# Shift and scale vectors of a two-block network: eight products with a column of ones in place of eight transposes and two VectorE sums

## The chip, the cores and the metric

One core of a Trainium2 chip runs the whole program. The metric is the device time of one execution in microseconds (us); smaller is better. The kernel before took 1699.3 us, the median of three runs (1696.49, 1699.3 and 1700.89). Three engines matter here: TensorE (PE in the rows; PEld is its weight load, which runs beside the product before it), VectorE (DVE) and ScalarE (ACT). GpSimd is POOL, SyncE is SP.

## The reference

The program is two networks in a row on an input x of 256 rows and 1024 columns, all in float32. The first has two blocks (an attention and gating mixer, then a convolution mixer), each followed by an MLP; the second is one block (attention with selection, then a feed-forward layer over many experts). What the change touches is the modulation, the same in each block:

```python
m = (silu(c) @ w_mod[l] + b_mod[l])[:, None, :]        # 6 * 1024 numbers
sh1, s1, g1, sh2, s2, g2 = jnp.split(m, 6, axis=-1)
h = rmsnorm(x, norm_g) * (1 + s1) + sh1                # ahead of the mixer
x = x + g1 * mixer(h)
h = rmsnorm(x, norm_g) * (1 + s2) + sh2                # ahead of the MLP
x = x + g2 * mlp(h)
```

c is one vector of 1024 numbers, so each of the six results is a vector of 1024.

## The kernel before, in words

A modulation vector is made in two stages. In `mod_steps` (line 286) POOL clears a tile t of 128 partitions by 2048 columns (line 294) and brings the bias into its first partition by a DMA (line 296); then eight steps follow, one per block k of 128 rows of the modulation weights. A step loads 128x1024 weights (line 142) and VectorE adds weights times silu(c) to t (line 306, `scalar_tensor_tensor`). Row p of t then holds the part of the sum that came from input rows p, p+128 and so on; what is left is a sum over the 128 partitions.

That last sum takes two forms. A gate (g1, g2) is wanted as a row that is the same on all partitions: `mod_row` (line 322) multiplies a 128x128 tile of ones by t (line 328) and ScalarE copies the result (line 329). A shift or a scale (sh, s) is wanted with its 1024 numbers down the partitions, as a tile of 128 partitions by 8 columns: that is `mod_cols` (line 310). For each of two halves it takes a PSUM tile `ps`, transposes four 128x128 blocks of t into it (line 318, `nc.tensor.transpose` with the identity `self.ident`), and VectorE sums each block along its columns (line 319, `tensor_reduce`). In a transpose and in a product alike, the block of t is the stationary operand that PEld loads; in a transpose the 128 columns of the identity stream past it.

`mod_cols` is called ten times: for sh2 and s2 of the first block from `steps` inside the attention mixer (`mixer0_rest`, lines 716 to 870), and eight times from `mod_groups` (line 335), whose `last` step (line 342) calls `mod_result` (line 332) for the two vectors of a group. `mod_groups` serves the two MLPs (`mlp`, line 592): in each, six vectors for what comes later are made between the products of the MLP itself, four of them by `mod_cols`.

The tiles named `ps` share eight PSUM banks; a tile that wants a bank waits until an earlier one has been read. The results go through `mod_scale` (line 394) for a scale, and are then read in `highs` (lines 425 and 427), where the normalised rows are scaled and shifted.

Around it: each weight matrix is brought in blocks, ScalarE makes its high part (line 172) and VectorE its low part (line 173), and every product is three matmuls, high by high, high by low and low by high (lines 179 to 181). In the attention mixer a score product (line 787) is followed by VectorE's sum with the bias and its minimum (line 627), ScalarE's exponential (line 629), VectorE's division (lines 632 and 634), transposes (line 803), copies (line 804) and value products (line 809).

The program's instructions are put into one queue per engine by a planner at build time. It prices each instruction and may send one ahead of another that stands earlier in the source when its operands are ready by its own clock, so the queues need not have the source's order. Each engine takes its queue in order.

Of the kernel before, what the change touches and what calls it, by code (L numbers as in the profile page):

```python
# [15 lines left out]
OP = mybir.AluOpType  # L16
AX = mybir.AxisListType
PSUM = bass.MemoryType.PSUM

P = 128  # L20
# [50 lines left out]
class Net:  # L71
# [238 lines left out]
    def mod_cols(self, t, half, name):  # L310

        nc = self.nc
        m = self.const([P, 8], name=name)
        for q in range(2):
            pt = self.ps([P, 4, P])
            for j in range(4):
                o = half * 1024 + (q * 4 + j) * P
                nc.tensor.transpose(pt[:, j, :], t[:, o : o + P], self.ident)
            nc.vector.tensor_reduce(m[:, q * 4 : q * 4 + 4], pt, axis=AX.X, op=OP.add)
        return m  # L320

    def mod_row(self, t, half):
# [1241 lines left out]
```

## Time and profile before

| | us |
|---|---|
| median of three runs | 1699.3 |
| profiled execution | 1695.26 |
| its span in the trace | 1693.5 |
| TensorE busy in the span | 1624.9 (96%) |
| VectorE busy | 1273.5 (75%) |
| ScalarE busy | 833.6 (49%) |
| GpSimd busy | 168.8 (10%) |
| granted TensorE clock, mean | 0.986 of full |

The span runs from the first to the last instruction of the trace, and 1.76 us of the profiled execution lie around it. Busy shares are means over stages with different limits, so what counts for an edit is the stage in which it lies. Matmuls are pipelined: the duration of one (273 ns, say) is longer than the distance at which the next one starts (0.11 us in the same run of instructions), so costs on TensorE are read from the distances between starts.

### The profile page before, as it was taken

What the parts mean: (1) busy time and instruction counts of PE and PEld (TensorE: products, weight loads), DVE (VectorE), ACT (ScalarE), POOL (GpSimd) and SP (SyncE); (2) the same over time, 40 slices, a digit from 0 to 9 for tenths busy, and PEclk for the clock granted to TensorE, in tenths of its full rate; (3) what the DMA queues carried; (4) which work ended last, traced back from release to release, by engine and by line L of the source; (5) the groups of instructions that cost most, each with busy time, mean ns of one, the idle gap of its engine ahead of it and who ended that gap; (6) DMA issues with size and microseconds to landing.
All of it is one profiled execution on the core that took longest, in us unless ns stands there. A gap on an engine that the chain in (4) does not pass through costs nothing.

```text
span 1693.5 us, 27346 instructions
## 1 busy us (share of the span) xinstructions
PE 1624.9 (96%) x10518; PEld 1444.4 (85%) x10518; DVE 1273.5 (75%) x2042; ACT 833.6 (49%) x1229; POOL 168.8 (10%) x133
## 2 busy tenths in 40 slices
PE   7998999999968999999989999999999999999998
PEld 4875898988857988886789999999999998888886
DVE  7887688876966888947869888988845556776665
ACT  6546545442126455646644455555554444444444
POOL 0110100000001000000047770000000000000001
PEclk9999999999979999999999999999999999999999
DMA  9783499956415999474166666777786668999970
GB/s 376 267 286 125 147 345 344 339 178 221 139 38 206 365 330 349 164 263 149 59 230 203 216 210 231 275 250 252 255 285 218 211 214 281 336 315 324 320 252 34
DMA packets 145397, 406.63 MB, mean 240 GB/s; under 512 B 13169, under 2 KB 46065, under 8 KB 143090
## 3 DMA queue, kind: packets, MB, share of 16 engines
q1 hardware_dynamic: 137280, 390.66, 67.0%
q10 hardware_dynamic: 7474, 14.16, 2.2%
q8 instruction: 82, 1.34, 0.3%
q14 instruction: 49, 0.40, 0.1%
q0 software_dynamic: 512, 0.07, 0.0%
HBM read 374.43 MB, written 30.41 MB: 239 GB/s over the span
## 4 chain that ended last, share of the span: by engine, by line
PE 75%; issue 10%; DVE 3%; ACT 2%; DMA 1%; POOL 1%; SPq 0%; POOLq 0%; DVEq 0%; ACTq 0%
PE ps L179 7%; PE ps L181 7%; PE ps L180 7%; PE pa L179 7%; PE pa L181 7%; PE pa L180 7%; PE acc L180 7%; PE acc L181 7%; PE acc L179 7%; PE acc L1309 3%; PE ps L588 2%; PE ps L894 2%; DVE m L885 1%; DMA st<-w_ff 1%; PE ps L1171 1%
## 5 line engine op out<-in xcount | busy, mean ns | idle before, releaser
L172 ACT CAST hi<-st 128x1024 fp32r<-128x1024 f32 x466 | 474.3, 1046 | 444.7 <-PE pa L180 169.6
L173 DVE TENSOR_TENSOR lo<-st,hi 128x1024 fp32r<-128x1024 f32 (+1 forms) x416 | 495.5, 1219 | 176.2 <-ACT hi L172 170.7
L179 PE MATMUL pa<-k,hi 128*128 128x256 f32 x1024 | 289.4, 283 | 0.0
L180 PE MATMUL pa<-k,hi 128*128 128x256 f32 x1024 | 286.3, 280 | 0.0
L181 PE MATMUL pa<-k,lo 128*128 128x256 f32 x1024 | 286.3, 280 | 0.0
L179 PE MATMUL ps<-k,hi 128*128 128x256 f32 x816 | 230.0, 283 | 0.0
L180 PE MATMUL ps<-k,hi 128*128 128x256 f32 x816 | 229.4, 281 | 0.0
L181 PE MATMUL ps<-k,lo 128*128 128x256 f32 x816 | 229.4, 281 | 0.0
L179 PE MATMUL acc<-hi,m 128*128 128x512 f32 x512 | 199.7, 390 | 0.0
L180 PE MATMUL acc<-lo,m 128*128 128x512 f32 x512 | 199.3, 389 | 0.1
L181 PE MATMUL acc<-hi,m 128*128 128x512 f32 x512 | 199.3, 389 | 0.0
L180 PEld LDWEIGHTS pa<-k,hi 128*128 128x128 f32 x1024 | 194.1, 190 | 0.5
L181 PEld LDWEIGHTS pa<-k,lo 128*128 128x128 f32 x1024 | 193.4, 189 | 0.0
L179 PEld LDWEIGHTS pa<-k,hi 128*128 128x128 f32 x1024 | 192.3, 188 | 0.5
L179 PEld LDWEIGHTS ps<-k,hi 128*128 128x128 f32 x816 | 154.2, 189 | 3.4 <-issue 1.0
L181 PEld LDWEIGHTS ps<-k,lo 128*128 128x128 f32 x816 | 156.2, 191 | 0.6 <-DVE lo L173 0.5
L180 PEld LDWEIGHTS ps<-k,hi 128*128 128x128 f32 x816 | 154.9, 190 | 2.1 <-issue 0.5
L173 POOL TENSOR_TENSOR lo<-st,hi 128x1024 fp32r<-128x1024 f32 x50 | 119.0, 2406 | 35.4 <-ACT hi L172 26.1
L306 DVE SCALAR_TENSOR_TENSOR k<-st,sil,k 128x1024 f32<-128x1024 f32 x96 | 117.6, 1280 | 0.0
L181 PEld LDWEIGHTS acc<-hi,m 128*128 128x128 f32 x512 | 96.1, 188 | 20.3 <-DVE m L195 0.4
L180 PEld LDWEIGHTS acc<-lo,m 128*128 128x128 f32 x512 | 96.1, 188 | 20.1 <-DVE lo L173 0.5
L179 PEld LDWEIGHTS acc<-hi,m 128*128 128x128 f32 x512 | 96.1, 188 | 19.6 <-issue 0.2
(298 smaller groups left out, 2623.4 us busy)
## 6 DMA issues: line engine op xcount, KB each, us to landing
st<-w_ff SPq DMA_DIRECT2D x128, 512.0 KB, 6.1
st<-uT SPq DMA_DIRECT2D x128, 512.0 KB, 4.6
st<-v SPq DMA_DIRECT2D x128, 512.0 KB, 5.3
st<-w_mod SPq DMA_DIRECT2D x96, 512.0 KB, 5.9
st<-w_ada SPq DMA_DIRECT2D x48, 512.0 KB, 5.9
st<-w_in SPq DMA_DIRECT2D x44, 512.0 KB, 5.7
gates<-k SPq DMA_DIRECT2D x16, 1024.0 KB, 7.4
k<-gates SPq DMA_DIRECT2D x16, 1024.0 KB, 8.5
```

The costliest lines, as they stand in the source:

```text
L172: nc.scalar.copy(h, raw)
L173: self.last_lo = (lo or nc.vector).tensor_tensor(l, raw, h.bitcast(F32), op=OP.subtract)
L179: mm(ps, l.hi, r.hi, start=first, stop=False)
L180: mm(ps, l.hi, r.lo, start=False, stop=False)
L181: mm(ps, l.lo, r.hi, start=False, stop=last)
L306: nc.vector.scalar_tensor_tensor(t[:, s], st, by, t[:, s], op0=OP.mult, op1=OP.add)
L588: mm(p[:, j, :], wt[k][:, j * P : (j + 1) * P], h[:, k, :], start=k == 0, stop=k == KC - 1)
L885: nc.vector.scalar_tensor_tensor(v, z[:, i : i + T], self.col("w_dw", c * 31 + i), v, op0=OP.mult, op1=OP.add)
L894: nc.tensor.matmul(yt[t][c % 2][:, c // 2 * P : c // 2 * P + P], z[:, t * P + i : t * P + i + P], dg[:, i, :], start=i == 0, stop=False)
L1171: nc.tensor.matmul(po[64 * i : 64 * i + 64, c * P :], v[:, c, (hd - 1 + i) * 64 : (hd + i) * 64], pTs[hd - 1 + i][:, 2 * c : 2 + c, :], st ...
L1309: nc.tensor.matmul(pg[:, i, :], y[:, q + i, :], z[:, q + i, :], start=True, stop=True)
```

## The change

Only `mod_cols` is changed. One PSUM tile of 128x8 takes the place of two tiles of 128x512; eight float32 matmuls, each with a block of t as stationary operand and the first column of the tile of ones as moving operand, take the place of eight transposes; each gives one column of the result, already summed over the partitions. One VectorE copy of 128x8 takes the place of two sums. The order of allocations in SBUF stays as it was (one `const` tile per call).

```diff
     def mod_cols(self, t, half, name):
 
         nc = self.nc
+        pt = self.ps([P, 8])
+        for j in range(8):
+            o = half * 1024 + j * P
+            nc.tensor.matmul(pt[:, j : j + 1], t[:, o : o + P], self.ones[:, 0:1], start=True, stop=True)
         m = self.const([P, 8], name=name)
-        for q in range(2):
-            pt = self.ps([P, 4, P])
-            for j in range(4):
-                o = half * 1024 + (q * 4 + j) * P
-                nc.tensor.transpose(pt[:, j, :], t[:, o : o + P], self.ident)
-            nc.vector.tensor_reduce(m[:, q * 4 : q * 4 + 4], pt, axis=AX.X, op=OP.add)
+        nc.vector.tensor_copy(m, pt)
         return m
```

## Rows read from the trace of the kernel before

**Rows 1.** Windows: stretch, us, busy PE PEld DVE ACT POOL (count), granted clock, DMA share, GB/s.
```profile
196.00:372.00 176.00, 175.49 (x1138) 158.65 (x1137) 146.61 (x140) 89.94 (x120) 2.77 (x3) 1.00 0.86 308
545.00:700.00 155.00, 155.00 (x1000) 140.09 (x1000) 132.28 (x124) 78.12 (x101) 2.77 (x3) 1.00 0.93 342
```

**Rows 2.** Line 318 alone: count, ns min/median/max, first and last start us, shape.
```profile
L318 PEld LDWEIGHTS ps<-ident,k x64: 139/141/143, 261.2 to 691.7; 128*128 128x128 f32 x64
L318 PE MATMUL ps<-ident,k x64: 272/273/273, 261.6 to 691.8; 128*128 128x128 f32 x64
```

**Rows 3.** Timeline of one MLP call: start us, us, engine, line, operation, count.
```profile
643.12 1.04 PE L318 MATMUL ps<-ident,k 128*128 128x128 f32 x8
643.99 1.88 PE L328 MATMUL ps<-k,ones 128*128 128x512 f32 x4
...
642.89 1.03 PEld L318 LDWEIGHTS ps<-ident,k 128*128 128x128 f32 x8
...
643.76 1.29 DVE L319 TENSOR_REDUCE s<-ps 128x4 f32<-128x512 f32 x2 [0.62 <-PE ps L318]
```

**Rows 4.** Groups by line: busy us, mean ns of one, idle before.
```profile
L319 DVE TENSOR_REDUCE s<-ps 128x4 f32<-128x512 f32 x10 | 6.5, 683 | 1.2 <-PE ps L318 1.2
L319 DVE TENSOR_REDUCE sh<-ps 128x4 f32<-128x512 f32 x10 | 6.4, 685 | 4.2 <-PE ps L318 4.2
```

**Rows 5.** Timeline of line 259: float32 products with two moving columns.
```profile
52.41 1.05 PE L259 MATMUL ps<-pairs,m 4*128 4x2 f32 x8
53.38 0.39 PE L179 MATMUL ps<-k,hi 128*128 128x256 f32 x1
```

**Rows 6.** Timeline of line 894: loads for full-height float32 products, 128 moving columns.
```profile
456.28 3.65 PEld L894 LDWEIGHTS ps<-diag,z 128*128 128x128 f32 x32 [1.69 <-issue]
```

**Rows 7.** Groups: weight loads of 4 and of 128 columns.
```profile
L248 PEld LDWEIGHTS ps<-m,silq 128*4 128x4 f32 x64 | 5.1, 88 | 11.0 <-DVE m L244 3.3 <-issue 1.7
...
L259 PEld LDWEIGHTS ps<-pairs,m 4*128 4x128 f32 x32 | 3.9, 186 | 3.8 <-DVE m L256 3.5 <-issue 0.4
```

**Rows 8.** Groups: a small VectorE instruction that reads PSUM.
```profile
L263 DVE TENSOR_TENSOR mc<-ps,cols 128x4 f32<-128x4 f32 x8 | 0.9, 158 | 3.3 <-PE ps L259 3.3
```

**Rows 9.** Timeline at the first attention call.
```profile
110.78 1.04 PE L318 MATMUL ps<-ident,mod 128*128 128x128 f32 x8
111.63 1.28 DVE L319 TENSOR_REDUCE sh<-ps 128x4 f32<-128x512 f32 x2
111.75 1.99 PE L787 MATMUL ps<-b,b 64*128 64x512 f32 x8
111.88 0.95 POOL L294 MEMSET mod<- 128x1024 f32 x1 [11.47 <-PE ps L318]
112.91 0.69 DVE L627 CUSTOM_DVE_ANT_1 m<-ps,bias 128x512 f32<-128x512 f32 x1
113.12 0.55 POOL L296 DMA_DIRECT2D mod<-b_mod  x1 [0.29 <-POOL mod L294]
113.66 0.19 PEld L179 LDWEIGHTS ps<-k,hi 128*128 128x128 f32 x1 [0.76 <-DVE sm L627]
...
116.52 1.29 DVE L306 SCALAR_TENSOR_TENSOR mod<-st,sil,mod 128x1024 f32<-128x1024 f32 x1 [0.83 <-POOL bias L780]
```

**Rows 10.** Instructions that use the tile `mod`: time of its DMAs to landing.
```profile
DMA to landing us min/median/max: 3.3/3.7/4.3
```

**Rows 11.** Timeline at the second attention call.
```profile
150.66 0.44 PE L318 MATMUL ps<-ident,mod 128*128 128x128 f32 x2
...
151.02 1.08 PE L809 MATMUL ps<-m,b 128*64 128x256 f32 x6
...
152.03 0.87 PE L318 MATMUL ps<-ident,mod 128*128 128x128 f32 x6
```

**Rows 12.** Chain of waits behind that call: start us, us, what.
```profile
153.43 1.07 ACT m L804 x2
...
158.31 2.35 DVE b L173 x2
```

## The prediction

> **What bounds the kernel now.** I read the busy shares first, then the stages in which the ten calls of `mod_cols` lie, then the neighbourhood of a call, then rows of like instructions for what the change adds. TensorE is busy for 96% of the span and VectorE for 75%. Eight of the ten calls lie in the two MLPs, four in each, the first from 261.6 us, the last with its last transpose at 691.8 [rows 2]. In the stretches that hold them TensorE is busy for 175.49 of 176.00 us and for 155.00 of 155.00 us at the full clock, while VectorE has 29.4 and 22.7 us to spare [rows 1]. The reader is to see that in these stretches only TensorE's own time counts: taking work from VectorE can win at most the 0.5 us in which TensorE is idle. The other two calls lie in the attention mixer, at 111 and 151 us, where several engines take turns in holding the others up.
>
> **What it removes.** 80 transposes and 20 sums. The transposes of one MLP call start at 643.12 and the next product starts at 643.99, so eight take 0.87 us, 0.109 each, though each lasts 0.273 [rows 2, 3]; 80 are 8.7 us of TensorE. The sums are 6.5 + 6.4 = 12.9 us of VectorE [rows 4].
>
> **What it adds to TensorE.** 80 float32 products of a 128x128 block of t with one column. The stationary block is the same as before; what goes is 127 of the 128 columns that stream past. So the question is what sets the distance from one product to the next, the stream or the load of the next block. The trace has no product with one column. The nearest rows are line 259's, with two columns: eight start from 52.41 and the next product follows at 53.38, 0.121 each with the change of operands at the end, and 0.114 within (1.05 for eight, less the last one's quarter microsecond, over seven) [rows 5]. They hold four partitions instead of 128, but 128 columns of weights, at the full clock. With all 128 partitions and 128 moving columns, line 894 loads 32 blocks in 3.65 us: less the last load's 0.19 that is 3.46 over 31, or 0.112 each [rows 6]. A plain load of 128 columns lasts 0.186 and one of four columns 0.088 [rows 7], so the 128 columns themselves take about 0.10: loads one behind the other make 0.11 whatever streams beside them. A transposing load is shorter, 0.141 [rows 2], which by the same subtraction is 0.053 of columns, and there it was the stream that made the 0.109. I take 0.112, nearest in partitions and in weights: 80 x (0.112 - 0.109) = +0.2 us. The ends are 0.121 (line 259 with its change-over, +1.0 us) and 0.053 (if plain loads came as fast as transposing ones, -4.5 us). TensorE is thus relieved of nothing: the stream that the change takes away was as long as the load that stays.
>
> Against this the Trainium skill has a rule (TensorE: Matmul & The Clock Gate, Back-to-back issue gap): a moving operand of 1 to 64 columns takes about 60 cycles, some 25 ns, from one product to the next, against 134 cycles at 128 columns. Its section LDWEIGHTS on the same page gives a load of 128 columns as 128/1.2, or 107 ns. By the first alone the 80 products would save 80 x (0.109 - 0.025) = 6.7 us; by the second nothing. Line 259's 0.114 speaks for the second.
>
> **What it adds to VectorE.** Ten copies of 128x8 out of PSUM. The nearest row reads 128x4 from PSUM and takes 0.158 [rows 8]: 1.6 us in all, so VectorE is relieved of 12.9 - 1.6 = 11.3 us, 9 of them in the MLPs, where its slack already covers everything. The copy waits for the eighth product where the first sum waited for the fourth transpose; behind it on VectorE stand the low parts of weights (line 173). At 643 the sums end at 645.0 [rows 3]; the copy would start at about 643.12 + 7 x 0.112 + 0.27 = 644.2 and end at 644.4, so those low parts come earlier, not later. TensorE did not wait for them before either.
>
> **PSUM.** A call takes one bank for a short while instead of two for longer, so no product waits longer for a bank. In the MLPs there is no such wait to remove, since TensorE is never idle.
>
> **The first attention call.** The two sums keep VectorE from 111.63 to 112.91, and then line 627 starts, though it needs only the first pair of the eight score products (line 787) that run from 111.75 to 113.74; by an estimate (a third of their 1.99 us) that pair was done at about 112.4. TensorE's next load comes at 113.66 and had waited 0.76 for line 627 [rows 9]. Here up to 0.5 us is to be had for both. It goes no further, however: the next step of the modulation (line 306) starts at 116.52 after VectorE had idled for 0.83 [rows 9]. The row names POOL, but POOL's bias DMA was issued at 113.12 and such DMAs take 3.3 to 4.3 us to land [rows 9, 10], so it was the landing, 116.4 or later. That DMA follows POOL's clearing of the tile at 111.88, which waits for the last transpose, and the last product ends at the same time as that. So VectorE meets the same landing again, and what it saved is idle time ahead of it. I take 0.1 us, with 0 and 0.5 as ends.
>
> **The second attention call.** TensorE does two transposes at 150.66, six value products, and six transposes at 152.03 [rows 11]; the chain then passes through ScalarE's copies (line 804) and later through VectorE's low part at 158.31 [rows 12]. The sums (0.68 each) are not on it. Fewer banks held may bring the transposes of line 803 forward; I take 0.2 us, with 0 and 0.7 (the time that one sum holds a bank longer) as ends.
>
> **Moves.** No DMA, POOL or SP instruction is added, removed or reordered in the source. The planner, however, puts the queues in order by its own clock, and it does leave the source's order: the eight transposes of one call stand in the queue as two and six around six products of line 809 [rows 11]. With cheaper steps it may choose other orders from 110 us on. In the MLPs an other order costs nothing while TensorE stays full. At stage ends it can shift a wait: the 2.35 us of the two low parts at 158.31 [rows 12] are one such wait, which may go or come again elsewhere, so I allow 2.4 us to either side.
>
> **The sum.** +0.2 - 0.1 - 0.2 = -0.1 us on the profiled execution's 1695.26. That execution lies 4.0 us below the median of 1699.3, and the three runs lie between 1696.5 and 1700.9; a change of -0.1 on the median gives 1699.2 us. A change of under 0.3% (5.1 us) can't be told from none with such runs.
>
> **Rivals.**
> 1. The products are cheaper than the load (loads hidden behind each other, or as fast as transposing ones). For it: 0.053 of columns in a transposing load [rows 2, 7]. Against it: lines 259 and 894 [rows 5, 6]. It gives -4.5 us at 0.053 each, 1694.8, so close to the 5.1 that with the spread of the runs half of it would be told as faster. Chance 0.06. By the page's rule on small moving operands above it would be 1692.6.
> 2. Slower: a plain float32 product can't overlap with the load of the next block as a transpose does. Each pair then costs 0.19 for the load alone, 80 x (0.19 - 0.109) = +6.5 us, 1705.7; with the product's 0.27 behind it, 0.46 and +28 us, 1727. It decides from 0.173 each, where 80 x 0.064 makes 5.1 us, and it sits where TensorE is full, with nothing to hide it. Against it are the 0.112 of line 894, plain, full height, a new load each [rows 6]. Chance 0.05. The Trainium skill has a rule that speaks for this rival (TensorE: Matmul & The Clock Gate, Terms): the transposing mode is four times faster for float32. By it a plain product would stand at 4 x 0.109 = 0.44, near the upper price; line 894's 0.112 against 0.109 disagrees.
> 3. The planner's new order decides, by over 5.1 us one way or the other, at stage ends that this trace can't foretell. Chance 0.10, half each way.
> 4. The 11.3 us of VectorE turn up in the time after all, because VectorE is what holds up the attention mixer: 1699.3 less at most the 1.2 us (0.5 and 0.7) of the two calls there, so this can't leave the bound of no change. It is part of the forecast.
>
> **How the numbers follow.** Forecast 0.79, rivals 0.06, 0.05 and 0.10. Faster by over 0.3%: 0.03 of rival 1 and 0.05 of rival 3, and 0.02 for the forecast's own tail, together 0.10. Slower: 0.05 and 0.05, together 0.10. Within: 0.80. The range joins the ends: down 4.5 (loads) and 1.2 (attention) from 1699.3, 1693.6; up 1.0 (change-over) and 2.4 (order), 1702.7, rounded up to 1703 for the spread of the runs.
>
> **What would show it.** In the profile after: ten groups of eight products in place of line 318 with 0.11 from start to start, loads of 0.19; ten VectorE copies of about 0.16 and VectorE some 11 us less busy; TensorE still full in both MLPs; line 306's start near 116.5 still tied to the bias DMA. The prediction is wrong if the products stand at 0.06 or at 0.19, if gaps open on TensorE in the MLPs, or if the stages after 180 us differ by more than 2 us with the same work.

## The result, and the profile after

| | before | after |
|---|---|---|
| median of four runs of each, us | 1697.89 | 1713.66 |
| lowest and highest, us | 1696.35 to 1700.89 | 1710.71 to 1715.89 |
| profiled execution, us | 1695.26 | 1711.66 |
| its span, us | 1693.5 | 1709.9 |
| TensorE busy, us | 1624.9 | 1641.8 |
| VectorE busy, us | 1273.5 | 1264.0 |
| granted TensorE clock, mean | 0.986 | 0.979 |

The change makes the kernel slower: ratio 1.0104, 95% interval 1.0081 to 1.0127. The prediction of 1699.2 us and its range (to 1703.0) are missed.

Lines of the changed kernel are one lower than before behind the change: the products stand on line 316, their copy on 318, the products of low parts still on 181, the relu on 600. First the page's line on the engines, then line 316 in the view of one line (count; ns minimum, median, maximum; first and last start; shape), and the copies from the groups by line:

```profile
PE 1641.8 (96%) x10598; PEld 1460.1 (85%) x10598; DVE 1264.0 (74%) x2032; ACT 834.3 (49%) x1229; POOL 168.8 (10%) x133
...
L316 PEld LDWEIGHTS ps<-ones,k x128: 187/192/193, 261.9 to 704.5; 128*128 128x128 f32 x128
L316 PE MATMUL ps<-ones,k x128: 165/250/251, 262.3 to 704.5; 128*128 128x1 f32 x128
L316 PEld LDWEIGHTS ps<-ones,mod x32: 186/192/193, 109.3 to 149.6; 128*128 128x128 f32 x32
L316 PE MATMUL ps<-ones,mod x32: 167/250/271, 109.7 to 149.6; 128*128 128x1 f32 x32
```

The reader is to see the counts. The source makes 80 products; the trace has 128 + 32 = 160 pairs of load and matmul. Before, the eight MLP calls had 64 records for 64 transposes [rows 2]. A product of two plain float32 operands is executed here as two passes, each with a load of its own; a transpose is one.

The second MLP call of the first MLP, in time (start, length, engine, line, count); it answers to [rows 3]:

```profile
308.29 1.84 PE L316 MATMUL ps<-ones,k 128*128 128x1 f32 x16
309.99 1.96 PE L327 MATMUL ps<-k,ones 128*128 128x512 f32 x4
...
310.17 0.17 DVE L318 COPY s<-ps 128x8 f32<-128x8 f32 x1 [1.85 <-PE ps L316]
310.37 0.17 DVE L393 SCALAR_TENSOR_TENSOR sm<-s,cols 128x8 f32<-128x8 f32 x1
310.45 1.22 DVE L173 TENSOR_TENSOR lo<-st,hi 128x1024 fp32r<-128x1024 f32 x1
```

Sixteen passes occupy TensorE from 308.29 to 309.99, 1.70 us or 0.106 a pass, 0.21 a product. The eight transposes of such a call occupied 0.87. VectorE's part of the call came out as forecast (0.17 a copy instead of 1.3 for two sums).

Each MLP has three calls: two for one vector and, last, one for two (sh2 and s2, "the double call"). This is what VectorE and TensorE do at the first double call, and then the same place in 2 us windows (length; busy time and count on PE, PEld, DVE, ACT, POOL; granted clock; DMA share; GB/s):

```profile
355.98 3.63 PE L316 MATMUL ps<-ones,k 128*128 128x1 f32 x32
359.47 0.36 PE L179 MATMUL ps<-k,hi 128*128 128x256 f32 x1
359.67 0.28 PE L180 MATMUL ps<-k,hi 128*128 128x256 f32 x1
361.01 0.58 PE L181 MATMUL ps<-k,lo 128*128 128x256 f32 x1 [1.06 <-DVE lo L173]
...
357.86 0.17 DVE L318 COPY sh<-ps 128x8 f32<-128x8 f32 x1 [3.28 <-PE ps L316]
359.65 0.17 DVE L318 COPY s<-ps 128x8 f32<-128x8 f32 x1 [1.62 <-PE ps L316]
359.73 1.22 DVE L173 TENSOR_TENSOR lo<-st,hi 128x1024 fp32r<-128x1024 f32 x1
```

```profile
356.00:358.00 2.00, 2.00 (x20) 2.00 (x19) 0.14 (x1) 2.00 (x3) 0.00 (x0) 1.00 1.01 414
358.00:360.00 2.00, 1.95 (x17) 1.75 (x16) 0.38 (x3) 0.35 (x1) 0.00 (x0) 1.00 0.39 160
360.00:362.00 2.00, 0.99 (x4) 0.99 (x5) 2.00 (x3) 0.00 (x0) 0.00 (x0) 0.52 0.12 18
362.00:364.00 2.00, 2.00 (x12) 2.00 (x11) 2.00 (x3) 0.00 (x0) 0.00 (x0) 0.50 0.78 225
364.00:366.00 2.00, 2.00 (x11) 2.00 (x11) 2.00 (x3) 0.00 (x0) 0.00 (x0) 0.50 0.73 246
366.00:368.00 2.00, 2.00 (x16) 2.00 (x15) 0.71 (x1) 0.00 (x0) 0.00 (x0) 0.77 0.13 45
```

Three things come together. The run of passes is 3.49 us long (355.98 to 359.47; the 16 transposes took 1.66). The copy of the second vector stands in VectorE's queue ahead of a low part of weights (line 173); VectorE idles 1.62 us for it, the low part starts at 359.73, and TensorE waits 1.06 us for that part. And behind the run the granted clock drops from 1.00 to 0.50, the 1.2 GHz level: by its means in the windows (0.52 and 0.77) from 360.1 to 366.9, 6.8 us, in which 11 or 12 products fall into a window of 2 us where cols128 below has 20. At 360.1 TensorE had been waiting for only 0.1 us, so the clock falls at the start of the wait and not behind it. Before, the same stage ran at 1.00 from end to end [rows 1].

**Where the 16.4 us lie.** ScalarE's relu and VectorE's last sum of an MLP (`m<-ps,grow`, line 459 before) come in the same number in both kernels, so their starts can be subtracted. First MLP, after minus before: 0.72 at its start, 0.71 ahead of the first call, 1.41 behind it, 2.08 behind the second, 7.88 at its end (387.42 against 379.54). Second MLP: 9.46 at its start, 9.60 ahead of the calls, then 10.31, 10.97, and 17.12 at its end. At the end of the kernel it is 16.4. So the four single calls cost 0.70 each, the double calls 5.80 and 6.15, and the stage between the MLPs 1.6. The 0.7 ahead of the first MLP is not the price of the two attention calls: at the end of that mixer (line 459's sum, at 187.27 in before) after is 0.95 ahead. It loses 1.7 from there to the first relu, where its granted clock is at 0.50 from 192.8 to 196.2 and that of before at 1.00; turncopy below, which keeps the transposes, has the same fall at 192.6 and loses the same 1.7. For the double calls the end of the MLP is the mark, since the next relu is misleading there: before, four later products had been drawn ahead of it.

### The profile page after: what moved, and what is told of

Same layout as the page of the kernel before. It is cut to its first block, busy times and chain, and to the rows that moved or that the text cites. A ratio compares the mean times of both kernels' runs of the same rounds, so it can differ in the third digit from the quotient of the medians.

```text
span 1709.9 us, 27500 instructions
## 1 busy us (share of the span) xinstructions
PE 1641.8 (96%) x10598; PEld 1460.1 (85%) x10598; DVE 1264.0 (74%) x2032; ACT 834.3 (49%) x1229; POOL 168.8 (10%) x133
## 4 chain that ended last, share of the span: by engine, by line
PE 75%; issue 10%; DVE 3%; ACT 1%; DMA 1%; POOL 1%; SPq 0%; POOLq 0%; ACTq 0%; DVEq 0%
PE ps L179 7%; PE ps L181 7%; PE ps L180 7%; PE acc L181 7%; PE acc L179 7%; PE acc L180 7%; PE pa L179 7%; PE pa L181 7%; PE pa L180 7%; PE acc L1308 3%; PE ps L587 2%; PE ps L893 1%; DVE m L884 1%; PE ps L1170 1%; PE ps L316 1%
```

## The experiments

Delays in this table are worked out in the same way against the trace of before: single call (mean of the four), first and second double call, and what the stage between the MLPs adds. "L510" is how long the eight products of the bias row in that stage take (line 510 before), which tells the clock there.

| kernel | ratio to before | single | double 1 | double 2 | between | L510 |
|---|---|---|---|---|---|---|
| after | 1.0104 [1.0081, 1.0127] | 0.70 | 5.80 | 6.15 | 1.6 | 7.19 |
| after_again | 1.0099 [1.0071, 1.0128] | 0.70 | 5.71 | 6.24 | 5.0 | 7.19 |
| cols128 | 1.0034 [1.0016, 1.0053] | 0.70 | 1.65 | 1.59 | -1.1 | 3.82 |
| split | 1.0062 [1.0038, 1.0087] | 0.70 | 3.24 | 3.85 | 3.9 | 7.19 |
| latecopy | 1.0088 [1.0060, 1.0115] | 0.70 | 5.67 | 6.20 | 4.9 | 7.19 |
| before_again | 0.9982 [0.9962, 1.0002] | 0.00 | 0.0 | 0.1 | 2.8 | 7.19 |
| turncopy | 0.9995 [0.9972, 1.0019] | 0.00 | 0.0 | 0.2 | 3.6 | 7.19 |
| late | 0.9994 [0.9978, 1.0010] | 0.00 | none | none | 1.4 | 4.01 |
| onepass | 1.0077 [1.0051, 1.0103] | 0.03, 2.74 | 4.37 | 2.79 | 4.6 | 7.19 |
| half4 | 1.0023 [1.0007, 1.0039] | -0.19 | 2.74 | 1.77 | 0.3 | 4.04 |
| one128 | 1.0046 [1.0028, 1.0063] | 0.02, 0.95 | 1.43 | 1.82 | -0.3 | 4.04 |
| after_late | 1.0057 [1.0039, 1.0075] | 0.70 | none | none | -1.3 | 3.84 |

Where two numbers stand for the single calls they are the means of the first and of the second call of each MLP, which differ. My theory after the result was: two passes per product, and at the double calls the clock, brought down by products that stream one column. The rivals: the place of the copy in VectorE's queue, the VectorE half of the change, or an accident of the planner's order.

**The change once more (after_again).** No edit.

> The changed kernel itself, beside the others on one chip. Its trace shows 160 loads and 160 products of line 316 where the source has 80 products, 0.107 us from one to the next. Theory 1 (two passes for each plain float32 product): 0.7 to 0.85 us more on TensorE at each of the ten calls, 7 to 8.5 us in all, in every execution. Theory 2 (two calls in a row, at 356 and 701 us): the clock is at half for some 6.5 us behind each pair of calls and TensorE waits about 1 us for a low part, together 3.4 us more for each pair, 6.8 in all. Theory 3 (the planner's order): the rest is spread over stage ends. Expected: ratio to before 1.008 to 1.0125. If the half clock in the stage of line 509 (500 to 510 us) is chance, it can be another there this time.

1716.09 us against 1694.01. The single calls cost 0.70 again, the double calls 5.71 and 6.24, with the wait of 1.1 us for the low part and the low clock at both. It repeats; what doesn't repeat is the stage between the MLPs (1.6, here 5.0, with one more fall of the clock, from 541.9 to 545.3).

**All 128 columns streamed (cols128).** Against the changed kernel:

```diff
-        pt = self.ps([P, 8])
-        for j in range(8):
-            o = half * 1024 + j * P
-            nc.tensor.matmul(pt[:, j : j + 1], t[:, o : o + P], self.ones[:, 0:1], ...)
...
-        nc.vector.tensor_copy(m, pt)
+        for q in range(2):
+            pt = self.ps([P, 4, P])
+            for j in range(4):
+                o = half * 1024 + (q * 4 + j) * P
+                nc.tensor.matmul(pt[:, j, :], t[:, o : o + P], self.ones, ...)
+            nc.vector.tensor_copy(m[:, q * 4 : q * 4 + 4], pt[:, :, 0])
```

> The products take all 128 columns of the tile of ones (every column then holds the sum), into two tiles of 128x512 as in the kernel before, and a VectorE copy takes one column of each. Passes as in the changed kernel, 160, and the distance from one to the next should stay at 0.107 to 0.112, since the load sets it; only the streamed columns are more. If the half clock behind the pairs of calls comes from streaming so few columns (theory 2a), it stays full here: 1698 + 8 = 1706, ratio 1.005 (the wait for the low part may remain). If it comes from the number of loads or from the pause behind them (theory 2b), the ratio stays at 1.009 to 1.0105.

1700.98 us, 1.0034. The double call of this kernel, and its windows:

```profile
356.08 3.73 PE L318 MATMUL ps<-ones,k 128*128 128x128 f32 x32
...
358.00:360.00 2.00, 2.00 (x20) 2.00 (x19) 1.52 (x4) 2.00 (x3) 0.00 (x0) 1.00 0.98 363
360.00:362.00 2.00, 2.00 (x20) 2.00 (x19) 1.97 (x4) 0.34 (x1) 0.00 (x0) 1.00 0.63 240
362.00:364.00 2.00, 2.00 (x20) 2.00 (x19) 2.00 (x3) 0.00 (x0) 0.00 (x0) 1.00 0.00 0
```

Thirty-two passes take as long as with one column (3.73 against 3.63), so the 127 columns more cost nothing: the loads set the distance, as the prediction had it. Now the clock stays at 1.00 and nothing waits for the low part, which here stood between the copies. What is left is the passes alone: 0.70 a single call and 1.65 and 1.59 for the double ones, 6.0 us in both MLPs. The ratio is below the 1.005 that I had expected with a full clock, since I had put the passes at 8 us. The edit removes two things at once, the few columns and the wait, so by itself it doesn't say which brought the clock down.

**The two vectors of the double call in two steps (split).** Against the changed kernel:

```diff
+            both = all(h[-1][0] == "s" for h in halves)
...
-                    r[n] = self.mod_result(n, box["t"], i)
+                    if not (both and i):
+                        r[n] = self.mod_result(n, box["t"], i)
...
+            if both:
+                def second(box=box, n=halves[1][-1]):
+                    results[-1][n] = self.mod_result(n, box["t"], 1)
+                steps.append(second)
...
-            want = len(steps) * max(b - 1, 0) // (nb - 3)
+            want = 24 * max(b - 1, 0) // (nb - 3)
```

> The changed kernel, with the second of the two vectors of the last group in each MLP (sh2, s2) made one block of the MLP later, so that no 32 passes stand in a row. Passes stay at 160. Theory 2 (a pair of calls in a row is what brings the clock down and the wait): 3 to 3.4 us less for each MLP, ratio 1.005 to 1.0065, and the clock stays at full through both MLPs. Theory 3 (order): no clear change from the changed kernel, 1.009 to 1.011.

1708.83 us, 1.0062. The planner put the second run only two products behind the first (356.61 and 358.63), which moved the low part ahead of the second copy. The wait is gone: TensorE is busy throughout, and yet the clock falls, for a shorter time:

```profile
358.49 0.17 DVE L318 COPY sh<-ps 128x8 f32<-128x8 f32 x1 [3.28 <-PE ps L316]
358.57 1.22 DVE L173 TENSOR_TENSOR lo<-st,hi 128x1024 fp32r<-128x1024 f32 x1
360.51 0.17 DVE L318 COPY s<-ps 128x8 f32<-128x8 f32 x1 [0.72 <-PE ps L316]
...
358.00:360.00 2.00, 2.00 (x20) 2.00 (x20) 1.30 (x2) 0.99 (x2) 0.00 (x0) 1.00 0.77 315
360.00:362.00 2.00, 2.00 (x14) 2.00 (x14) 1.45 (x4) 0.00 (x0) 0.00 (x0) 0.68 0.58 156
362.00:364.00 2.00, 2.00 (x11) 2.00 (x11) 2.00 (x3) 0.00 (x0) 0.00 (x0) 0.50 0.68 188
364.00:366.00 2.00, 2.00 (x19) 2.00 (x18) 2.00 (x3) 0.00 (x0) 0.00 (x0) 0.97 0.55 199
```

So the wait is not needed for the fall. Beside the 1.65 of the passes the first double call costs 1.6 here; with the wait, in the changed kernel, 2.6 us more than that. The ratio lies where theory 2 had put it, but not for its reason: the clock was to stay full, and it fell at both double calls.

**The copies of the double call a step later (latecopy).** Against the changed kernel:

```diff
+                if both:
+                    box["pt"] = self.ps([P, 2, 8])
...
+                    return
...
+            if both:
+                def second(box=box, halves=halves):
+                    for i, h in enumerate(halves):
+                        m = results[-1][h[-1]] = self.const([P, 8], name=h[-1])
+                        self.nc.vector.tensor_copy(m, box["pt"][:, i, :])
+                steps.append(second)
```

> The changed kernel, with the 16 products of the last group still in a row (32 passes) into one PSUM tile, and their two VectorE copies issued one block of the MLP later, so that no low part of a weight waits behind a copy. If the wait of about 1 us for the low part is what brings the clock down (theory 2b), clock and wait are both gone: ratio 1.005 to 1.0065. If the 32 passes with one column do it (theory 2a), the clock still falls behind them and only the wait goes: 1 us less for each pair, ratio 1.008 to 1.0095.

1713.46 us, 1.0088: as the changed kernel. The planner issued the copies as early as before (the first at 359.32 after 5.07 us of VectorE waiting for the passes), and the wait of 1.06 stayed. The edit didn't do what it was made for and tells nothing on its question.

**The kernel before once more (before_again).** No edit.

> The kernel before once more, for its clock in the stage from 475 to 510 us. Theory: the half clock of line 509 (510 in this kernel) in the changed kernel is not the change's own: that stage has pauses of TensorE ahead of it and its clock falls in the kernel before too, at another point in another execution. Then the eight bias products of line 510 take 3.8 us in some executions and up to 7.2 in others, and the stage from 400 to 530 us differs by some us between two traces of the same kernel. If it is the change's own, they take 3.8 us here again.

1695.41 us, 0.9982. The stage between the MLPs took 2.8 us more than in the first trace of the same kernel, without any change. Its end is where: the products of the bias row (first the first trace of before, then this one, then the changed kernel),

```profile
493.27 3.82 PE L510 MATMUL ps<-m,ones 1*128 1x512 f32 x8
```

```profile
492.68 7.19 PE L510 MATMUL ps<-m,ones 1*128 1x512 f32 x8
...
492.00:496.00 4.00, 4.00 (x8) 1.84 (x7) 1.52 (x4) 3.85 (x10) 0.00 (x0) 0.50 0.00 0
```

```profile
500.26 7.19 PE L509 MATMUL ps<-m,ones 1*128 1x512 f32 x8
```

They ran at 0.50 here and in the changed kernel, and mostly higher in the first trace of before. The 1.6 us that the changed kernel lost in this stage can't be put down to the change. I can't exclude that the change makes the low clock there more likely: all five kernels that lose the clock at both double calls show 7.19, but before_again and turncopy, which never lose it in the MLPs, show it too.

**The VectorE half alone (turncopy).** Transposes stay; the copy of one column takes the place of the sum, so the sum over the other columns is left out.

```diff
-            nc.vector.tensor_reduce(m[:, q * 4 : q * 4 + 4], pt, axis=AX.X, op=OP.add)
+            nc.vector.tensor_copy(m[:, q * 4 : q * 4 + 4], pt[:, :, 0])
```

> VectorE's half of the change alone: the 80 transposes stay, each of the 20 VectorE sums is replaced by a copy of one column out of four (the sum over the other columns is left out). VectorE is relieved of 12.9 - 20 x 0.16 = 9.7 us, TensorE does as before. Theory of the prediction (VectorE's relief is worth nothing where TensorE is full): ratio 0.9985 to 1.0015. Rival (the relief is worth its time, or the planner's new order costs): off by 3 us or more, under 0.998 or over 1.002.

1696.08 us, 0.9995. VectorE is relieved of 9.7 us (20 copies of 0.16 instead of 12.9 us of sums) and the time doesn't move: the MLPs differ by 0.0 to 0.2 us. That half of the prediction held.

**The double call elsewhere, with transposes (late).** sh2 and s2 are made where they are first needed, in the convolution mixer and at the end of attention.

```diff
+    def late(self, mods):
+        t, names = mods.pop("late")
+        for i, n in enumerate(names):
+            mods[n] = self.mod_result(n, t, i)
...
+                if all(h[-1][0] == "s" for h in halves):
+                    results[-1]["late"] = box["t"], [h[-1] for h in halves]
+                    return
...
```

> The kernel before with its transposes and sums, but the two vectors of the last group of each MLP (sh2, s2) made only where they are needed: ahead of the normalisation in the convolution mixer and at the end of the second block's attention, where TensorE has pauses. What is tried is whether the cost of a call on the full TensorE can be taken off the path: 2 x 1.74 = 3.5 us less, ratio 0.998, if the pauses take it up; 1.000 if the new places lie on the path as well.

1695.89 us, 0.9994: the MLPs get 1.75 and 1.16 us shorter (16 transposes took 1.66), the later stages longer, and nothing is left that can be measured.

**One pass per product (onepass).** VectorE first rounds the sums into a stage buffer of the type fp32r, and the products are of that type, with two columns of ones; the low parts of the sums are left out. Against the changed kernel:

```diff
+        tr = self.wp.tile([P, D], F32R, tag="st", name=self.nm("tr"), bufs=STAGES)
+        nc.vector.tensor_copy(tr, t[:, half * D : (half + 1) * D])
-        pt = self.ps([P, 8])
+        pt = self.ps([P, 8, 2])
...
-            nc.tensor.matmul(pt[:, j : j + 1], t[:, o : o + P], self.ones[:, 0:1], ...)
+            nc.tensor.matmul(pt[:, j, :], tr[:, j * P : (j + 1) * P], self.onesr, ...)
...
```

> The products of the change in one pass instead of two: VectorE first copies the 128x1024 half of t into the type of the high parts (the low part is left out of the result), and each block is multiplied with two columns of ones of that type; one copy of 128x8 as in the change. TensorE has 80 loads and products again. Theory 1 (two passes per plain float32 product are the main cost): TensorE's part at a call is 0.87 us as with transposes, the delay at the MLP calls is gone, and with 16 passes instead of 32 behind each other the clock stays full in both MLPs: ratio 0.999 to 1.003. If few columns as such were the cost, the ratio stays above 1.005.

1710.22 us, 1.0077: my expectation fell. At the first single call of each MLP it holds: eight records, and a delay of 0.03 instead of 0.70, so the price of a single call is the number of passes. But the buffer is taken from the ring through which the weights come, and at the second call TensorE waits for their parts (1.62 and 0.76 us; the delay is 2.74). And at the double call the run of 16 passes is no longer than one of 16 transposes (1.70 against 1.66), and the clock falls all the same, in a wait of 1.26 us (and in one of 1.06 at the second double call):

```profile
361.48 0.58 PE L181 MATMUL ps<-k,lo 128*128 128x256 f32 x1 [1.26 <-DVE lo L173]
...
358.00:360.00 2.00, 2.00 (x19) 1.96 (x18) 0.24 (x2) 1.87 (x3) 0.00 (x0) 1.00 1.04 418
360.00:362.00 2.00, 0.74 (x4) 0.54 (x4) 1.97 (x4) 0.64 (x1) 0.00 (x0) 0.67 1.02 395
362.00:364.00 2.00, 2.00 (x12) 2.00 (x11) 2.00 (x3) 0.00 (x0) 0.00 (x0) 0.50 1.08 317
```

So it may be the wait after all, or the few columns. The next kernel changes only the columns.

**One pass per product, 128 columns (one128).** Against the last one:

```diff
-            nc.tensor.matmul(pt[:, j, :], tr[:, j * P : (j + 1) * P], self.onesr, ...)
+                by = tr[:, (q * 4 + j) * P : (q * 4 + j + 1) * P]
+                nc.tensor.matmul(pt[:, j, :], by, self.onesr[:, 0:1].to_broadcast([P, P]), ...)
...
```

> The kernel of the one-pass products (the sums first rounded by VectorE into a stage buffer, low parts left out) with 128 columns of ones streamed in each of the 80 products instead of 2, read from one column by a stride of zero. Each product is still one load and one pass. The one with 2 columns lost about 3.3 us at the first double call with the clock at 0.50 from 361 to 367 us, although its run was 1.84 us long, and 2.7 us at the second single call, where TensorE waited for parts of weights. Theory 1 (few columns bring the clock down): the clock is 1.00 from 354 to 370 us, the double call costs 0 to 1.5 us, the wait at the second single call remains since the stage buffer is taken all the same; ratio 1.002 to 1.006. Theory 2 (the wait for the low part brings it down, whatever is streamed): TensorE waits about 1.2 us at 360 us as it did with 2 columns and the clock falls behind it again; ratio 1.006 to 1.009.

1700.55 us, 1.0046. The wait is there, a little longer, and the clock holds:

```profile
350.86 1.89 PE L322 MATMUL ps<-onesr,tr 128*128 128x128 f32 x16
...
354.35 0.39 PE L181 MATMUL ps<-k,lo 128*128 128x256 f32 x1 [1.30 <-DVE lo L173]
...
352.00:354.00 2.00, 1.05 (x9) 0.84 (x8) 1.40 (x5) 1.47 (x2) 0.00 (x0) 1.00 0.99 367
354.00:356.00 2.00, 1.65 (x14) 1.65 (x15) 2.00 (x3) 0.00 (x0) 0.00 (x0) 1.00 0.96 373
```

The two kernels differ in the columns that are streamed (and in two PSUM tiles and two copies of four results where one took eight). Waits of 1.30 and 1.10 us with 128 columns ahead of them leave the clock at 1.00 at both double calls; waits of 1.26 and 1.06 with two columns ahead of them go with a fall at both. So theory 1 is right that the columns decide. The double calls of this kernel cost 1.43 and 1.82, with those waits in them. The profiled execution is the fastest of the six (1694.37; the others 1699.1 to 1705.7), so the trace doesn't show what the median lost.

**Half the products (half4).** Against the changed kernel: four blocks of each vector instead of eight; the other four are left out.

```diff
-        pt = self.ps([P, 8])
-        for j in range(8):
+        pt = self.ps([P, 4])
+        for j in range(4):
...
```

> Products of four of a vector's eight blocks of 128 rather than of all eight (the other four blocks of the vector are left out; the copy writes the four results twice). That is 8 passes per vector instead of 16, so 16 at the double call, and nothing else differs from the changed kernel. Theory 1 (a price per pass, about 0.107 us, which the 8 transposes of a vector had too, and a falling clock only behind the run of 32 one-column passes of 3.6 us): the single calls cost between -0.1 and +0.1 us against the kernel before, the double call too, the granted clock stays at 1.00 from 354 to 370 us, ratio 0.998 to 1.001. Theory 2 (not the length of the run but the copy standing in VectorE's queue ahead of a low part makes TensorE wait, and the wait brings the clock down): the single calls cost nothing but the double calls still cost 2 to 4 us each with the clock at 0.50 behind them, ratio 1.002 to 1.005.

1698.55 us, 1.0023, inside what theory 2 gave and above what theory 1 gave. The passes now number as the transposes did, and the single calls cost -0.19. The double calls still cost 2.74 and 1.77: TensorE waits 1.06 us for the low part at both. At the first the clock falls at the end of that wait (for less long), at the second it holds:

```profile
356.00:358.00 2.00, 0.94 (x8) 0.74 (x7) 1.50 (x4) 0.99 (x2) 0.00 (x0) 0.96 0.72 287
358.00:360.00 2.00, 2.00 (x10) 2.00 (x11) 2.00 (x2) 0.00 (x0) 0.00 (x0) 0.50 0.59 164
360.00:362.00 2.00, 2.00 (x14) 2.00 (x14) 2.00 (x3) 0.00 (x0) 0.00 (x0) 0.68 0.65 215
...
694.00:696.00 2.00, 1.84 (x16) 1.64 (x15) 0.63 (x3) 2.00 (x3) 0.00 (x0) 1.00 0.98 393
696.00:698.00 2.00, 1.10 (x9) 1.11 (x10) 2.00 (x3) 0.02 (x1) 0.00 (x0) 1.00 0.35 104
698.00:700.00 2.00, 2.00 (x20) 2.00 (x20) 2.00 (x2) 0.00 (x0) 0.00 (x0) 1.00 0.83 277
```

So a run of 16 passes (1.7 us) with one column doesn't always cost the clock: with full work behind it (the single calls of the changed kernel's MLPs) it stayed at 1.00, with a wait behind the run it fell once and once not, and with a second such run two products later it fell without a wait (split). Theory 1 was wrong in asking for the long run, and theory 2 in making the wait enough: at the second double call the wait is there and the clock holds. Over all kernels, at the double calls in the MLPs: with one or two columns the clock fell at 11 of 12 (after, after_again, split, latecopy, onepass, half4), with 128 columns at none of 4 (cols128, one128), with transposes at none of 6 (before, before_again, turncopy). What the few columns need beside them to cost the clock stays open.

**The changed kernel with the double call elsewhere (after_late).** The edit of "late", made to the changed kernel.

> The changed kernel with the shift and scale of the second MLP half (sh2, s2, the double call) made where they are first used, in the convolution mixer and at the end of attention, in place of in the MLP. Theory 1 (0.70 us for each single call, over 4 us for the double call in the MLP because of the clock behind it and the wait): the MLPs are 4 to 5 us each shorter than in the changed kernel, and what the moved calls cost at their new places is not known from any run with products, but the same move with transposes cost nothing in all; ratio to the kernel before 1.001 to 1.006. Theory 2 (the double call costs what it costs wherever it stands): ratio 1.007 to 1.011.

1704.15 us, 1.0057, inside what theory 1 gave. The MLPs keep the 0.70 of their single calls and otherwise are those of "late" to 0.02 us, at a clock of 1.00. The long run now lies in the convolution mixer (32 passes at 457.45). The clock falls behind it there too (0.85 from 460 to 462, 0.50 from 462 to 464), but the time from the first MLP's end to the second's start isn't longer than in before (-1.3). The second long run, at the end of the second block's attention (32 passes at 846.91), has a fall behind it as well (850.5 to 853.9). From the second MLP's end to that attention's last sums this kernel's trace loses 6.0 us against before; that of late, with transposes and no such fall, loses 5.5 there, those of the kernels that leave the call in the MLP between -2.3 and +0.8. So in these single traces that place is no cheaper than the MLP, whatever makes the vectors. Of the some 17 us that the changed kernel loses 7 to 8 are gone by moving this call; this is still slower than before.

None of these kernels beats the kernel before.

## Why the prediction was wrong, point by point

**What bounds the kernel now** held: in the MLPs only TensorE's time counts, and relieving VectorE brought nothing there (turncopy).

**What it adds to TensorE** is the step that failed, in its count. It took 0.112 for a product, from rows that give the distance between loads. That distance came out right: 0.112 from start to start within a run, or 0.106 to 0.109 when the length of a run is shared out, and one column or 128 make no difference to it (cols128). But a plain float32 product is two such passes, 0.215 as the mean over the MLP calls, so the term is 80 x (0.215 - 0.109) = +8.5 us where the sum had +0.2. The rows cited had it in plain sight: the groups count 32 loads for line 259 [rows 7], whose source makes 16 products, and the eight records at 52.41 [rows 5] are four products of a call. I read records as products, and never divided the one by the other. The same holds for line 894 [rows 6]. The transposes, one record each [rows 2], made the two look alike. A page that the prediction didn't weigh speaks for passes: the Trainium skill (FP8 and Floating Point Precision, TensorE Precision Notes) says that a true float32 product goes through the array four times. The trace of before agrees where 512 columns stream: the two float32 products of a gate (line 328) are four records [rows 3], 0.43 us from one load to the next, so 0.86 a product, against 0.23 from start to start for a matmul of rounded parts with 512 columns (lines 179 and 180), nearly four times:

```profile
642.43 0.39 PE L179 MATMUL ps<-hi,m 128*128 128x512 f32 x1
642.66 0.39 PE L180 MATMUL ps<-lo,m 128*128 128x512 f32 x1
...
644.43 0.19 PEld L328 LDWEIGHTS ps<-k,ones 128*128 128x128 f32 x1 [0.24 <-issue]
644.86 0.19 PEld L328 LDWEIGHTS ps<-k,ones 128*128 128x128 f32 x1 [0.24 <-issue]
```

With one column the traces show two passes at 0.106 to 0.109 and no more. In the MLPs the term measured 4 x 0.70 + 1.65 + 1.59 = 6.0 us (cols128), for 64 of the 80 products.

**The rivals.** The second, slower from 0.173 a product, is what happened, at 0.215, for another reason than the one it named: loads do overlap with products, there are two of each. It had a chance of 0.05. Its evidence against, "a new load each" in line 894, was the misreading. The Trainium skill's rule named there (TensorE: Matmul & The Clock Gate, Terms), that the transposing mode is four times faster for float32, points the right way; here it is 0.215 against 0.109, a factor of two. Its formula for a load (same page, LDWEIGHTS) gives 128/1.2 = 107 ns for 128 columns; the trace agrees, with 0.106 to 0.109 a pass.

**What it adds to VectorE** failed at the double calls. The single copy was costed as if it started right behind a short run ("those low parts come earlier, not later"). Where two vectors follow each other, the second copy stands ahead of a low part for as long as 16 passes take, 1.62 us of idle VectorE at 359.65, and TensorE waits 1.06 for that part (0.96 at the second double call). The prediction looked at one call, at 643, which is a call for one vector; the double calls have another neighbourhood. The relief itself was as good as worthless, as forecast (turncopy); VectorE's busy time fell by 9.5 us, a little less than the 11.3 forecast.

**The clock** wasn't a term at all: the prediction named the full clock of the MLPs and took it to stay, without a reason. What the double calls cost beside their passes is 5.80 - 1.65 = 4.15 us and 6.15 - 1.59 = 4.56: about 1 us of it the wait, the rest, by subtraction, the 6.8 us at half the clock. Split keeps the fall without the wait, a shorter one, at 1.6 and 2.3.

**The attention calls** can't be read from single traces. After was 0.95 us ahead of before behind them (at 187 us), where 0.3 was forecast; the other kernels stand between 3.6 ahead (one128) and 1.5 behind (after_again) at that place. One reading failed: line 627 (626 after) was not held up by the sums. It starts 1.16 us behind the first score product in both traces (112.91 - 111.75 and 112.61 - 111.45), in after with VectorE idle for 0.89 us before it, so the estimate of a third of 1.99 us was too short and those 0.5 us were not to be had. Line 306 started at 115.31 rather than the 116.5 of "What would show it": the bias DMA landed in 2.1 us in this execution, in 3.3 in that of before, and VectorE came straight from line 626. The prediction had tied it to a landing at 116.4 or later.

**Moves** were allowed 2.4 us either way. The stage between the MLPs alone varied by 2.8 us between two traces of the kernel before.

The sum as it should have been: passes 8.5 by their distances (6.0 measured in the MLPs), double calls another 8.7, against 15.8 us between the medians. In the traces the MLPs' share is 6.0 + 8.7 = 14.7 of 16.4 us; the 1.6 of the stage between them stays open. The passes could be read from the trace of before; the rest could not, in its size.

## What to carry to other kernels

Divide the records of a line by the instructions in its source before using the distance between records as a price: a plain float32 product here is two loads and two passes, a transpose of the same block one. Where TensorE is the bound, a product that streams one column cost here what its loads cost, and a row of them can cost the clock behind it as well. With 128 columns the row took no longer here, and the clock held; single runs of 16 passes with full work behind them kept it too. A copy that waits for products belongs in the queue behind whatever those products' successors wait for.

## What the runs showed of the hardware that was not expected

- Passes with 1 and with 128 columns, each with a load of 128 columns, take the same time (3.49 us for 32, or 0.109 each, in both the changed kernel and cols128).
- A float32 product with 512 columns is two records 0.43 us apart, where matmuls of rounded parts with 512 columns stand 0.23 apart (lines 328 and 179 of before).
- Passes of one column count as busy in the profile (2.00 of 2.00 us from 356 to 358), but behind 32 of them the granted clock fell from 1.00 to 0.50, the 1.2 GHz level, and came back 6.8 us later, while TensorE was busy with full products. Behind 32 passes of 128 columns it stayed at 1.00.
- In one128 TensorE was busy for only 1.05 of 2.00 us from 352 to 354, with 128 columns ahead, and kept its clock; in onepass it was busy for 0.74 from 360 to 362, with two columns ahead, and lost it.
